# A hybrid attention block on one core: two gate parts moved ahead, four weight splits moved to GpSimd, weight scaling and late loads moved in the last stage

## The chip, the cores and the metric

The kernel runs on one core of a Trainium2 chip. The metric is the device time of one execution in microseconds. The kernel's text is Python that issues instructions to five engines: TensorE (PE, products), VectorE (DVE, `V` in the code), ScalarE (ACT, `A`), GpSimd (POOL, `G`) and SyncE (SP, `SY`), whose queue starts nearly all DMAs. All data is fp32.

## The reference

One layer of a diffusion backbone over 512 latent tokens of width 1024, with 256 context tokens.

```python
mod = silu(c) @ w_ada + b_ada
sh1, sc1, gt1, sh2, sc2, gt2 = split(mod, 6)
h = modulate(rms_norm(x, norm1_g), sh1, sc1)
mix = merge_branches(o_mla @ w_br_mla, gla_branch(o_gla, gr, ...), gate_logits, w_out)
x = x + gt1 * mix                         # the two branches: latent attention, gated linear attention
h = modulate(rms_norm(x, norm2_g), sh2, sc2)
val, gate = split(h @ w_up, 2)            # d_ff = 2816
hid = gelu(conv3x3(gate)) * val
x = x + gt2 * (hid @ w_down)
return rms_norm(x, final_g)
```

`gt2`, the "second gate", is the last sixth of the modulation vector: 1024 numbers, each a sum over the 1024 rows of a column of `w_ada`.

## The kernel before

**Split products.** Each fp32 operand is kept as two tiles of a rounded type, a high part `h` and the rest `l`. `split(hi, lo, src, eng)` makes them: a cast on ScalarE (`A.copy`, the CAST rows), then a subtraction `lo = src - hi` on `eng`, GpSimd by default and VectorE where `V` is given. `mm3` multiplies with three products. A weight goes by DMA into a `raw` (or `rawd`) tile, is split into `whi` and `wlo` (or into two `s4` tiles, named `s`), and is then used by TensorE.

**Order of the work.** From the linear attention on, a planner fixes each engine's order ahead of time: the text's order gives priority, and the planner puts an instruction where it expects its operands and buffers to be ready. On the chip each engine then runs its list strictly in order. `tc.issue_after(ins)` holds the instructions of a block behind `ins` on the queue of `ins`; `load[0]` is the last weight load that was marked so.

**The stages around the change.**

- *Linear attention* (pool `eg`, 217 to 408 us): four heads `h`. Each makes decays, states, output and gate on VectorE and ScalarE while TensorE runs the projections. In between come `mod_begin` and `mod_end` (other sixths of the modulation: two 512 KB loads and eight multiply-adds on VectorE each) and the first half of the merge, `merge_mla(j)`, for j = 0 to 7; the last head does `merge_mla(6)` and `merge_mla(7)`.
- *Merge* (pool `em_`, from 408 us): for j = 0 to 7 the second half of the merge, with weights loaded one step ahead by `merge_weights`; some of `w_out` is loaded here (`load_wo`), and the first gate `gt1` is made.
- *`w_out` and the second norm*: `w_out_norm(t)` for four token tiles t: 48 products of width 512, then on VectorE `xn = p * gt1`, `x += xn` in two halves, the sum of squares on ScalarE, the root, and `xn = x * r`. `transposed(t, n)` turns that `xn` on TensorE and modulates it.
- *Up projection and convolution* (559 to 772 us), per block of 128 columns: two projections, nine convolution steps on VectorE (`ac<-pb,cwT,ac`), gelu, product.
- *Last stage* (from 772 us): NP = 9 pairs of blocks of `w_down` in a seven-product scheme, the sums of weights having been written to device memory earlier (`ws`). A first loop over n makes four of the products from `wa` and `wb` (two splits each), a second one (`back`, with `back_weights(n)`) the other three. The last NL = 4 blocks are multiplied plainly by weights that `load_down` scales by `gt2` beforehand (`raw<-raw,gt`). `x2`, stored in device memory after `w_out_norm`, is loaded again and the result added; `fg` is the gain of the final norm.

**The second gate.** `gt2` is a 128 x 1024 tile, zero but for the bias in row 0. `gate_part(j)` adds 256 columns to it: two loads of 512 KB into `wa` tiles (two buffers) and eight multiply-adds `gt<-wa,csilu,gt` on VectorE, so 8 loads and 32 multiply-adds in all for the four parts. In the up projection, at i = 12, TensorE sums it over the partitions. Parts 0 and 1 stand in the merge (at j = 6 and after the last `load_wo`), part 2 after `w_out_norm(0)`, part 3 after `w_out_norm(1)`:

```python
n0 = w_out_norm(0)
gate_part(2)
n1 = w_out_norm(1)
gate_part(3)
transposed(0, n0)
n0 = w_out_norm(2)
```

Of the kernel before, what the change touches and what calls it, by code (L numbers as in the profile page):

```python
# [9 lines left out]
F32 = mybir.dt.float32  # L10
# [3 lines left out]
ALU = mybir.AluOpType  # L14
# [9 lines left out]
NF = FF // 128  # L24
NL = 4
# [47 lines left out]
def block_kernel(ctx: ExitStack, tc: tile.TileContext, p, out):  # L73
# [80 lines left out]
    def k3(t_, k, n):  # L154
        return t_[:, 0:k * n].rearrange("p (k n) -> p k n", k=k)
# [150 lines left out]
    def mod_begin(tile_, acc=None):  # L306
        begun.append(mod_part(3072 + len(begun) * 256, mp_tile() if acc is None else acc, tile_))
# [782 lines left out]
    gt1 = S4([128, 1024], F32)  # L1090
    G.dma_start(out=gt1, in_=p["b_ada"][0:1, 2048:3072].broadcast_to([128, 1024]))

    with tc.tile_pool(name="egl", bufs=1) as eg:
        smask = LF[:, 768:1024].bitcast(mybir.dt.bfloat16)
        pinned.add("G")
# [170 lines left out]
        def gate_out(h, on, gr):  # L1266
            tp = pb()
            for t in range(4):
                cs = slice(t * 128, (t + 1) * 128)
                PE.transpose(tp[:, cs], on[:, cs], ident)  # L1270
            V.scalar_tensor_tensor(out=gr, in0=tp, scalar=col("gla_norm_g", 0), in1=gr, op0=ALU.mult, op1=ALU.mult)
            yT[h] = S4([128, 2, 512])
            split(yT[h][:, 0, :], yT[h][:, 1, :], gr, V)

        def merge_mla(j):
            wga = split_w(load_cols(w_in, CGA + j * 128))
            ga = pb()
            proj(wga, ga)
            sg = tl(eg, [128, 512], F32, "sg", 1)
            sigmoid(sg, ga)  # L1280
            wbm = split_w(load_cols(w_brm, j * 128, k1=4), 512)
            bm = pb()
            for k in range(4):
                mm3(bm, k3(wbm[0], 4, 128)[:, k, :], k3(wbm[1], 4, 128)[:, k, :], oT[k][:, 0, :], oT[k][:, 1, :], k == 0,
                    k == 3)
            if j % 2 == 0:
                m1[j // 2] = S4([128, 2, 512], F32)
            tt(V, m1[j // 2][:, j % 2, :], bm, sg, ALU.mult)
# [13 lines left out]
        for h in range(GH):  # L1302
            St = states(h, dec)
            on = output(h, dec, Q, St)
            if h + 1 < GH:
                dec = decay(h + 1)
                merge_mla(2 * h)
                kq = proj_kq(h + 1)
                with tc.issue_after(key_end[0].ins):
                    mod_end()  # L1310
            else:
                merge_mla(2 * h)
                mod_end()
                mod_begin(S4f)
                merge_mla(2 * h + 1)
            gate_out(h, on, gr)
            if h + 1 < GH:
                Q = apply(kq, dec)
                gr = gate(h + 1)
                to_tokens(dec, Q)  # L1320
                mod_begin(S4f)
                merge_mla(2 * h + 1)
# [4 lines left out]
    hbm = ctx.enter_context(tc.tile_pool(name="hbm", bufs=1, space=bass.MemoryType.DRAM))  # L1327
    x2_ = [tl(hbm, [128, 1024], F32, f"x2_{t}") for t in range(4)]
    sums_ = [tl(hbm, [128, 2048], F32, f"ws_{i}") for i in range(NP)]
    gate_ = ctx.enter_context(tc.tile_pool(name="gate", bufs=1))  # L1330
    gt2 = tl(gate_, [128, 1024], F32, "gt2")
    V.memset(gt2, 0.0)
    SY.dma_start(out=gt2[0:1, :], in_=p["b_ada"][0:1, 5120:6144])
    emf_ = tc.tile_pool(name="emf", bufs=1)
    emf = emf_.__enter__()
    x2 = [tl(emf, [128, 1024], F32, f"x2{t}") for t in range(4)]
# [22 lines left out]
    with tc.tile_pool(name="emg", bufs=1) as em_:  # L1359
# [3 lines left out]
        def mraw():  # L1363
            return tl(em_, [128, 1024], F32, "xn", 3)


        def gate_part(j):
            acc = gt2[:, j * 256:j * 256 + 256]
            for k0 in (0, 4):
                r3 = k3(tl(em_, [128, 1024], F32, "wa", 2), 4, 256)  # L1370
                SY.dma_start(out=r3, in_=w_ada[:, k0:k0 + 4, 5120 + j * 256:5376 + j * 256])
                for k in range(4):
                    V.scalar_tensor_tensor(out=acc, in0=r3[:, k, :], scalar=csilu[:, k0 + k:k0 + k + 1], in1=acc,
                                           op0=ALU.mult, op1=ALU.add)

        gsum = p2()
        ahead = merge_weights(0)
        for j in range(8):
            wgb, wbg = ahead
            gb = pb()  # L1380
            proj(wgb, gb)
            if j + 1 < 8:
                ahead = merge_weights(j + 1)
            bg = pb()
            for k in range(4):
                bg_ = mm3(bg, k3(wbg[0], 4, 128)[:, k, :], k3(wbg[1], 4, 128)[:, k, :], yT[k][:, 0, :], yT[k][:, 1, :], k == 0,
                    k == 3)
            sg = tl(em_, [128, 512], F32, "sg", 2)
            si = sigmoid(sg, gb)
            tt(V, sg, bg, sg, ALU.mult)  # L1390
            tt(V, sg, sg, m1[j // 2][:, j % 2, :], ALU.add)
            mg[j] = S4([128, 2, 512])
            split(mg[j][:, 0, :], mg[j][:, 1, :], sg, V)
            ahead_ = load[0].ins
            if j in (1, 2, 3, 5):
                load_wo(len(wo), mraw)
            if j == 0:
                mod_end()
            with tc.issue_after(ahead_):
                if j < 4:  # L1400
                    mod_part(2048 + j * 256, gsum[:, j * 256:j * 256 + 256], mraw)
                elif j == 4:
                    mod_begin(mraw, p2()[:, 0:256])
            if j == 6:
                m_, gh, gl = mp_tile(), *[tl(em_, [128, 1024], F32R, "xn", 3) for _ in range(2)]
                with tc.issue_after(si.ins):
                    A.copy(m_, begun[7])
                    A.copy(gh, gsum)
                sub(V, gl, gsum, f(gh))
            elif j == 7:  # L1410
                with tc.issue_after(bg_.ins):
                    mod_fin(7, m_)
                    gp = p2()
                    for half in range(2):
                        hs = slice(half * 512, (half + 1) * 512)
                        total(gp[:, hs], gh[:, hs], gl[:, hs])
                        tt(V, gt1[:, hs], gt1[:, hs], gp[:, hs], ALU.add)
            if j == 6:
                with tc.issue_after(load[0].ins):
                    gate_part(0)  # L1420
        for k in range(4, 8):
            load_wo(k)
        with tc.issue_after(load[0].ins):
            gate_part(1)
        h2h = [S4([128, 2, 512]) for _ in range(4)]
        h2l = [S4([128, 2, 512]) for _ in range(4)]
        def w_out_norm(t):
# [31 lines left out]


        n0 = w_out_norm(0)
        gate_part(2)
        n1 = w_out_norm(1)
        gate_part(3)
        transposed(0, n0)
        n0 = w_out_norm(2)
        transposed(1, n1)
# [24 lines left out]
    with tc.tile_pool(name="eff", bufs=1) as ef:  # L1492
# [104 lines left out]

        def back_weights(n):
            r = back_raw(n)
            SY.dma_start(out=r, in_=w_down[:, 2 * n + 1, :])  # L1600
            w = back_hl(n)
            split(*w, r, V)
            if n % 2 == 0:
                k = min(2, NP - n)
                r = back_raw(n)
                for i in range(k):
                    SY.dma_start(out=r[:, 512 * i:512 * i + 512], in_=sums_[n + i][:, 1024:1536])
                h_, l_ = back_hl(n)
                split(h_[:, 0:512 * k], l_[:, 0:512 * k], r[:, 0:512 * k], V)
                t4[0] = h_, l_  # L1610
            h_, l_ = S4([128, 768]), S4([128, 768])
            split(h_, l_, second[n], V)
            return w, t4[0], (h_, l_)
# [6 lines left out]
        for n in range(NP):  # L1620
            r = raw_()
            SY.dma_start(out=r[:, 0:512], in_=w_down[:, 2 * n, 0:512])
            SY.dma_start(out=r[:, 512:1024], in_=sums_[n][:, 1536:2048])
            wa = split_w(r, eng=V)
            r = raw_()
            SY.dma_start(out=r, in_=sums_[n][:, 0:1024])
            wb = split_w(r, eng=V)
            a, z = n == 0, n == NP - 1
            product(p1, first[n], 0, wa, 0, a, z)
            product(p6, first[n], 768, wa, 512, a, z)  # L1630
            product(p7, first[n], 512, wb, 512, a, z)
            product(p5, first[n], 256, wb, 0, a, z)
            if n in (2, 4, 6, 8):
                r = load_down(NF - NL + n // 2 - 1)
                wl_.append((S4([128, 1024]), S4([128, 1024])))
                split(*wl_[-1], r, V)
            if n == NP - 3:
                bw.append(back_weights(0))
# [20 lines left out]
                    product(p3, w[2], 256, w[0], 512, n == 0, z)  # L1659

        x2 = [S4f() for _ in range(4)]
        for t in (2, 3, 0, 1):
            SY.dma_start(out=x2[t], in_=x2_[t])
        SY.dma_start(out=fg, in_=p["final_g"].rearrange("(a b) -> a b", a=1).broadcast_to([128, 1024]))
        for n in range(NP):
            if n:
                bw.append(back_weights(n))
            if n < NP - 2:
                back(n, (2, 4, 3), bw[n])
        for x in (2, 4, 3):  # L1670
# [110 lines left out]
```

## Time and profile before

| | |
|---|---|
| median of 3 runs | 893.69 us (892.61 to 893.79) |
| the profiled execution | 892.85 us |
| its span, first to last instruction | 891.1 us |
| mean granted TensorE clock | 0.993 |
| busy: TensorE, weight loads, VectorE, ScalarE, GpSimd | 869.7, 738.1, 642.8, 412.2, 374.0 us |
| DMA | 130.53 MB, 146 GB/s on average |

Rows of the profile name tiles by the program's names without numbers, as out<-in: `gt` is a gate tile, `wa` a gate part's weights, `xn` a scratch tile of the merge, `p` and `pb` tiles of the product memory. A releaser is what ended an engine's idle time. Several helpers record their instructions under one line, L90, so a row is told apart by its tiles and its time. A product's end in the trace is modelled; starts are what to go by.

### The profile page before, as it was taken

What the parts mean: (1) busy time and instruction counts of PE and PEld (TensorE: products, weight loads), DVE (VectorE), ACT (ScalarE), POOL (GpSimd) and SP (SyncE); (2) the same over time, 40 slices, a digit from 0 to 9 for tenths busy, and PEclk for the clock granted to TensorE, in tenths of its full rate; (3) what the DMA queues carried; (4) which work ended last, traced back from release to release, by engine and by line L of the source; (5) the groups of instructions that cost most, each with busy time, mean ns of one, the idle gap of its engine ahead of it and who ended that gap; (6) DMA issues with size and microseconds to landing.
All of it is one profiled execution on the core that took longest, in us unless ns stands there. A gap on an engine that the chain in (4) does not pass through costs nothing.

```text
span 891.1 us, 12819 instructions
## 1 busy us (share of the span) xinstructions
PE 869.7 (98%) x4794; PEld 738.1 (83%) x4794; DVE 642.8 (72%) x1054; ACT 412.2 (46%) x666; POOL 374.0 (42%) x253
## 2 busy tenths in 40 slices
PE   7999999999999999999999899999999999999996
PEld 5788899888888888888888689888888888877785
DVE  4477788876978686845775984986677666877867
ACT  4355676773454645433544333433334333356514
POOL 2512355460624343423743422877768776000005
PEclk9999999999999999999999899999999999999998
DMA  9960001225414242427982930756546755467702
GB/s 292 319 178 1 1 4 34 72 69 168 106 40 133 55 131 58 119 80 262 266 267 91 278 104 17 235 168 194 190 155 195 232 168 193 144 201 275 255 13 95
DMA packets 141648, 130.53 MB, mean 146 GB/s; under 512 B 7947, under 2 KB 122995, under 8 KB 141586
## 3 DMA queue, kind: packets, MB, share of 16 engines
q1 hardware_dynamic: 140354, 126.67, 46.4%
q10 hardware_dynamic: 832, 2.40, 0.7%
q8 instruction: 37, 0.61, 0.3%
q0 software_dynamic: 400, 0.65, 0.2%
q14 instruction: 25, 0.20, 0.1%
HBM read 115.87 MB, written 13.63 MB: 145 GB/s over the span
## 4 chain that ended last, share of the span: by engine, by line
PE 80%; DVE 7%; DMA 6%; ACT 4%; issue 2%; POOL 1%; SPq 0%; DVEq 0%; ACTq 0%; POOLq 0%
PE pb L90 42%; PE p L90 17%; PE pb L89 14%; PE p L89 6%; DMA raw<-in_w_ada_dram 2%; DVE s L90 2%; ACT s L90 2%; DMA wa<-in_w_ada_dram 1%; DVE gt L90 1%; DMA s<-ws 1%; DVE wlo L90 1%; DMA xn<-in_w_ada_dram 1%; ACT P L90 1%; DVE mx L90 0%; POOL s L90 0%
## 5 line engine op out<-in xcount | busy, mean ns | idle before, releaser
L90 POOL TENSOR_TENSOR wlo<-raw,whi 128x1024 fp32r<-128x1024 f32 (+1 forms) x88 | 200.7, 2290 | 226.5 <-ACT whi L90 193.2
L90 PE MATMUL pb<-s,whi 128*128 128x512 f32 (+1 forms) x906 | 271.3, 382 | 0.0
L90 PEld LDWEIGHTS pb<-s,whi 128*128 128x128 f32 x906 | 167.3, 188 | 32.3
L90 PE MATMUL pb<-s,wlo 128*128 128x512 f32 (+1 forms) x453 | 172.7, 381 | 0.0
L90 ACT CAST whi<-raw 128x1024 fp32r<-128x1024 f32 (+1 forms) x105 | 101.8, 973 | 126.2 <-PE pb L90 49.1
L90 DVE SCALAR_TENSOR_TENSOR ac<-pb,cwT,ac 128x441 f32<-128x441 f32 (+2 forms) x160 | 110.9, 694 | 11.4 <-ACT ac L90 7.4
L89 PE MATMUL pb<-s,whi 128*128 128x512 f32 x320 | 101.2, 394 | 0.0
L90 PEld LDWEIGHTS pb<-s,wlo 128*128 128x128 f32 x453 | 85.2, 188 | 16.3
L90 PE MATMUL p<-s,s 128*128 128x512 f32 (+1 forms) x398 | 86.8, 371 | 1.0 <-DVE s L90 0.9
L90 PEld LDWEIGHTS p<-s,s 128*128 128x128 f32 x398 | 68.4, 193 | 14.5 <-DVE s L90 2.0
L89 PEld LDWEIGHTS pb<-s,whi 128*128 128x128 f32 x320 | 59.3, 188 | 11.5
L89 PE MATMUL pb<-s,wlo 128*128 128x512 f32 x160 | 62.8, 392 | 0.0
L90 POOL TENSOR_TENSOR s<-s,edge 128x512 f32<-128x512 f32 x7 | 12.1, 1759 | 114.7 <-ACT s L90 114.7
L90 PE MATMUL p<-whi,s 128*128 128x512 f32 x168 | 56.3, 394 | 0.0
L90 PE MATMUL pb<-whi,s 128*128 128x512 f32 x164 | 53.7, 390 | 0.0
L90 ACT ACTIVATE ac<-ac 128x512 f32<-128x512 f32 x22 | 13.9, 632 | 77.5 <-DVE ac L90 77.5
L90 PE MATMUL pb<-s,s 128*32 128x128 f32 (+2 forms) x340 | 46.3, 319 | 0.9 <-DMA s<-in_w_ada_dram 0.9
L90 DVE TENSOR_TENSOR pl<-pb,ph 128x512 fp32r<-128x512 f32 x48 | 33.0, 687 | 13.0 <-ACT ph L90 12.5
L90 PE MATMUL p<-kT,s 128*128 128x512 f32 (+1 forms) x192 | 41.2, 350 | 0.9 <-ACT P L90 0.9
L90 PEld LDWEIGHTS pb<-s,s 128*128 128x128 f32 (+1 forms) x340 | 36.1, 159 | 6.8 <-DVE rv L90 1.3
L90 PE MATMUL p<-s,whi 128*128 128x256 f32 (+1 forms) x156 | 38.6, 338 | 0.0
L90 ACT CAST ph<-pb 128x512 fp32r<-128x512 f32 x48 | 28.2, 587 | 20.7 <-PE pb L90 20.5
(274 smaller groups left out, 1667.6 us busy)
## 6 DMA issues: line engine op xcount, KB each, us to landing
raw<-in_w_up_dram SPq DMA_DIRECT2D x44, 512.0 KB, 5.9
raw<-in_w_in_dram SPq DMA_DIRECT2D x28, 512.0 KB, 4.1
rawd<-in_w_down_dram SPq DMA_DIRECT2D x21, 512.0 KB, 5.8
s<-in_w_ada_dram SPq DMA_DIRECT2D x20, 512.0 KB, 6.3
ws<-rawd SPq DMA_DIRECT2D x18, 512.0 KB, 5.6
raw<-in_w_ada_dram SPq DMA_DIRECT2D x10, 512.0 KB, 7.6
xn<-in_w_ada_dram SPq DMA_DIRECT2D x10, 512.0 KB, 4.8
raw<-in_w_down_dram SPq DMA_DIRECT2D x9, 512.0 KB, 4.4
```

The source lines that it names most:

```text
L89: return fn(*args, **kw)
L90: ins = fn(*args, **kw)
```

## The change

The gate's zeroing (now on GpSimd), bias load and `gate_part` move ahead of the linear attention, and `gate_part` takes the pool for its `wa` tiles. Part 0 now stands in the last head between `mod_begin` and `merge_mla(7)`, part 1 behind `merge_mla(7)`, part 2 at j = 6 of the merge, part 3 after the last `load_wo`; none stands between the `w_out_norm` calls. In the last stage the low parts of `wa` and `wb` of the pairs 0 and 1 are made on GpSimd, `load_down` comes at the pairs 1, 2, 4, 5 instead of 2, 4, 6, 8, and the loads of `x2` and `fg` come after `back_weights(5)` (NP - 4 = 5) instead of before the second loop.

```diff
+    gate_ = ctx.enter_context(tc.tile_pool(name="gate", bufs=1))
+    gt2 = tl(gate_, [128, 1024], F32, "gt2")
+    G.memset(gt2, 0.0)
+    SY.dma_start(out=gt2[0:1, :], in_=p["b_ada"][0:1, 5120:6144])
+
+    def gate_part(j, pool):
+        acc = gt2[:, j * 256:j * 256 + 256]
+        for k0 in (0, 4):
+            r3 = k3(tl(pool, [128, 1024], F32, "wa", 2), 4, 256)
+            SY.dma_start(out=r3, in_=w_ada[:, k0:k0 + 4, 5120 + j * 256:5376 + j * 256])
+            for k in range(4):
+                V.scalar_tensor_tensor(out=acc, in0=r3[:, k, :], scalar=csilu[:, k0 + k:k0 + k + 1], in1=acc,
+                                       op0=ALU.mult, op1=ALU.add)
...
                 mod_begin(S4f)
+                with tc.issue_after(load[0].ins):
+                    gate_part(0, eg)
                 merge_mla(2 * h + 1)
+                with tc.issue_after(load[0].ins):
+                    gate_part(1, eg)
...
-    gt2 = tl(gate_, [128, 1024], F32, "gt2")
-    V.memset(gt2, 0.0)
-    SY.dma_start(out=gt2[0:1, :], in_=p["b_ada"][0:1, 5120:6144])
...
             if j == 6:
                 with tc.issue_after(load[0].ins):
-                    gate_part(0)
+                    gate_part(2, em_)
         for k in range(4, 8):
             load_wo(k)
         with tc.issue_after(load[0].ins):
-            gate_part(1)
+            gate_part(3, em_)
...
         n0 = w_out_norm(0)
-        gate_part(2)
         n1 = w_out_norm(1)
-        gate_part(3)
         transposed(0, n0)
...
         def back_weights(n):
             r = back_raw(n)
-            SY.dma_start(out=r, in_=w_down[:, 2 * n + 1, :])
+            load[0] = SY.dma_start(out=r, in_=w_down[:, 2 * n + 1, :])
...
-            wa = split_w(r, eng=V)
+            wa = split_w(r, eng=G if n < 2 else V)
             r = raw_()
             SY.dma_start(out=r, in_=sums_[n][:, 0:1024])
-            wb = split_w(r, eng=V)
+            wb = split_w(r, eng=G if n < 2 else V)
...
-            if n in (2, 4, 6, 8):
-                r = load_down(NF - NL + n // 2 - 1)
+            if n in (1, 2, 4, 5):
+                r = load_down(NF - NL + len(wl_))
                 wl_.append((S4([128, 1024]), S4([128, 1024])))
                 split(*wl_[-1], r, V)
...
-        for t in (2, 3, 0, 1):
-            SY.dma_start(out=x2[t], in_=x2_[t])
-        SY.dma_start(out=fg, in_=p["final_g"].rearrange("(a b) -> a b", a=1).broadcast_to([128, 1024]))
         for n in range(NP):
             if n:
                 bw.append(back_weights(n))
+            if n == NP - 4:
+                with tc.issue_after(load[0].ins):
+                    for t in (2, 3, 0, 1):
+                        SY.dma_start(out=x2[t], in_=x2_[t])
+                    SY.dma_start(out=fg, in_=p["final_g"].rearrange("(a b) -> a b", a=1).broadcast_to([128, 1024]))
```

More of the change, by code (lines that the diff above doesn't have):

```diff
@@ L1329, in block_kernel @@
     sums_ = [tl(hbm, [128, 2048], F32, f"ws_{i}") for i in range(NP)]
-    gate_ = ctx.enter_context(tc.tile_pool(name="gate", bufs=1))
-    gt2 = tl(gate_, [128, 1024], F32, "gt2")
-    V.memset(gt2, 0.0)
-    SY.dma_start(out=gt2[0:1, :], in_=p["b_ada"][0:1, 5120:6144])
     emf_ = tc.tile_pool(name="emf", bufs=1)
@@ L1364, in mraw @@
             return tl(em_, [128, 1024], F32, "xn", 3)
[L1367 to L1374, printed above, removed]
         gsum = p2()
```

## The prediction

> **What bounds the kernel now.** I read the page first, then TensorE's own waits, then TensorE's and VectorE's timelines around the longest of them, then the windows for the granted clock.
>
> ```profile
> span 891.1 us, 12819 instructions
> PE 869.7 (98%) x4794; PEld 738.1 (83%) x4794; DVE 642.8 (72%) x1054; ACT 412.2 (46%) x666; POOL 374.0 (42%) x253
> ```
>
> TensorE is busy for 869.7 of 891.1 us. The change alters no product, so it can only gain where TensorE waits or runs at a lower clock, and it can lose at any place where TensorE does not wait now. The waits, from the view by releaser: the first row is of the whole run, the next three of the window from 750 us on.
>
> ```profile
> PE pb L90 <- DVE xn L90: 3.7, 1, 3.7
> ...
> PE p L90 <- DVE wlo L90: 0.8, 1, 0.8
> PE p L90 <- DVE s L90: 0.4, 1, 0.4
> PE pb L90 <- DVE wlo L90: 0.2, 1, 0.2
> ```
>
> One wait stands out, 3.7 us for `xn`, the normalised token tile that `transposed(0, n0)` turns. The three last-stage waits make 1.4 us. TensorE's timeline around the long one (start, length, tiles, count, idle before), one row of the chain for an undisturbed rate, and the windows (busy of PE, PEld, DVE, ACT, POOL, then clock, DMA share, GB/s):
>
> ```profile
> 475.47 5.60 PE L90 MATMUL p<-s,s 128*128 128x512 f32 x24
> ...
> 481.38 23.11 PE L90 MATMUL p<-s,s 128*128 128x512 f32 x100
> 508.19 1.97 PE L90 MATMUL pb<-cst,xn 128*128 128x128 f32 x8 [3.71 <-DVE xn L90]
> 509.81 11.10 PE L90 MATMUL p<-s,s 128*128 128x512 f32 x39
> 520.75 1.03 PE L90 MATMUL pb<-cst,xn 128*128 128x128 f32 x8
> ...
> 564.66 108.83 PE pb L90 x480
> ...
> 500.00:510.00 10.00, 6.29 (x29) 5.19 (x28) 9.82 (x17) 2.40 (x5) 3.21 (x2) 0.86 0.84 255
> 510.00:520.00 10.00, 10.00 (x37) 8.10 (x37) 9.89 (x27) 4.05 (x9) 0.00 (x0) 0.80 0.33 104
> ```
>
> The wait costs twice. After it the granted clock is 0.86 and 0.80. An undisturbed product takes 108.83/480 = 0.227 us; the 39 after the wait take 520.75 - 509.81 = 10.94 us instead of 39 x 0.227 = 8.84, and the 8 transposes 1.97 us instead of the 1.03 of the next eight. That is 2.1 + 0.9 = 3.0 us of slow clock, so this place costs 3.7 + 3.0 = 6.7 us. VectorE is 98 to 99% busy there. Its timeline:
>
> ```profile
> 488.70 4.13 DVE L90 SCALAR_TENSOR_TENSOR gt<-wa,csilu,gt 128x256 f32<-128x256 f32 x8
> ...
> 493.95 2.09 DVE L90 TENSOR_TENSOR x<-x,xn 128x512 f32<-128x512 f32 x1
> 496.98 1.60 DVE L90 SCALAR_TENSOR_TENSOR gt<-wa,csilu,gt 128x256 f32<-128x256 f32 x1 [0.95 <-DMA wa<-in_w_ada_dram]
> 498.50 2.88 DVE L90 TENSOR_TENSOR x<-x,xn 128x512 f32<-128x512 f32 x1
> ...
> 507.40 0.74 DVE L90 TENSOR_SCALAR xn<-x,rr 128x1024 f32<-128x1024 f32 x1
> ...
> 508.65 0.68 DVE L90 TENSOR_TENSOR x<-x,xn 128x512 f32<-128x512 f32 x1
> ...
> 489.00:514.00 25.00, 13.63 (x23) 0.00 (x0) 0.86 0.93 270
> ...
> 493.07 7.75 POOL L90 TENSOR_TENSOR wlo<-raw,whi 128x1024 fp32r<-128x1024 f32 x3 [8.04 <-ACT whi L90]
> ```
>
> The reader sees the gate's multiply-adds (`gt<-wa`) threaded through the chain that makes `xn`; the window row, of the instructions on `gt` alone, gives them 13.63 of 25 us (23 of them). The first eight are `gate_part(1)`, the rest parts 2 and 3. While GpSimd splits (493 to 501 us), VectorE's operations on two SBUF tiles are slow: 2.09 and 2.88 us for one that takes 0.68 after it.
>
> **The change part by part.**
>
> *Gate parts out of the `w_out_norm` calls.* After the change one part stands before `w_out_norm(0)`, where part 1 stands now (the eight at 488.70 stay), and none between the calls. Sixteen multiply-adds and four 512 KB loads leave this stretch. So `xn` comes sooner: the `x` update that ended at 496.0 is followed at once by the second, 0.68 to 2.88 us, ending at 496.7 to 498.9. From the squares to `xn` I take the undisturbed chain of `w_out_norm(3)`:
>
> ```profile
> 530.94 1.06 ACT L90 ACTIVATE xn<-x 128x1024 f32<-128x1024 f32 x1 [6.05 <-DVE x L90]
> ...
> 533.34 0.76 DVE L90 TENSOR_SCALAR xn<-x,rr 128x1024 f32<-128x1024 f32 x1
> ```
>
> 534.1 - 530.9 = 3.2 us, and 0.2 for the two hand-overs between engines, an estimate from the 0.05 us between the end of `xn` at 508.14 and the transposes: `xn` stands ready at 500.1 to 502.3. TensorE's queue as it is reaches the transposes at 508.19 - 3.71 = 504.5, so with this order the wait is gone with 2 to 4 us to spare. But the order is written by a planner, which with less vector work may put the transposes further ahead. Two calls have 96 products, so 24 + 100 - 96 = 28 products of `w_out_norm(2)` stand before the transposes now, 6.4 us; if all of them go behind, TensorE is there at 498.1 and waits 2.0 to 4.2 us. Bounds of the remaining wait: 0 and 4.2, with up to 3.0 of slow clock. I take 2.0. The planner's order was 3.7 us too early over a chain with four slow operations: 2.09, 2.88, 1.60 and 2.23 (the longest of the multiply-adds, in the row by tile below) make 8.8 us where 0.68, 0.68 and twice that row's median of 0.49 make 2.3, so 6.5 too much. The two that stay have 3.6 of that, and 3.7 x 3.6/6.5 = 2.0. I charge no slow clock for 2.0: of the two waits here that are nearest in size, 3.7 had it and the 0.8 us below had not (clock 1.00 from 780 to 790), and the bounds keep it. Term: -6.7 + 2.0 = -4.7, between -6.7 and +0.5.
>
> [...]
>
> *Parts 0 and 1 into the last head of linear attention.* Sixteen multiply-adds on VectorE, four 512 KB loads on SP's queue, two new `wa` buffers there:
>
> ```profile
> L90 DVE SCALAR_TENSOR_TENSOR gt<-wa,csilu,gt x32: 472/485/2227, 461.1 to 516.0; 128x256 f32<-128x256 f32 x32
> ...
> 390.00:400.00 10.00, 10.00 (x59) 8.71 (x57) 2.02 (x7) 3.96 (x8) 2.38 (x1) 1.00 0.07 21
> 400.00:410.00 10.00, 10.00 (x49) 8.32 (x49) 7.71 (x16) 3.69 (x6) 4.52 (x3) 1.00 0.57 173
> ```
>
> 16 x 0.49 = 7.8 us against 10.3 us of idle VectorE from 390 to 410; DMA is 7% and 57% busy. I cost it at nothing. If the cover is gone, one multiply-add stuck behind GpSimd (2.23 us at most) ahead of a state update can hold TensorE once: 0 to +2.2. What queues behind the new loads on SP is the merge stage's weights, the slower rival below. A gain is excluded here, since TensorE is busy for 10.00 of 10 us in both rows. Parts 2 and 3 take the places of parts 0 and 1 with the same instructions: nothing. The memset and the bias row go ahead of the stage, onto GpSimd and SP:
>
> ```profile
> 226.33 7.35 POOL L90 TENSOR_TENSOR wlo<-raw,whi 128x1024 fp32r<-128x1024 f32 x3 [29.88 <-ACT whi L90]
> ...
> 411.69 0.91 DVE L90 MEMSET gt<- 128x1024 f32 x1 [0.35 <-DVE s L90]
> ```
>
> GpSimd is idle for 29.88 us there, which covers it; without cover it would be the memset's 0.91 us.
>
> *Last stage.* The four splits of pairs 0 and 1 go from VectorE to GpSimd, and the scaled weights (load, multiply, split) from pairs 2, 4, 6, 8 to 1, 2, 4, 5:
>
> ```profile
> L90 POOL TENSOR_TENSOR wlo<-raw,whi 128x1024 fp32r<-128x1024 f32 x70 | 177.4, 2539 | 168.2 <-ACT whi L90 134.8 <-PE pb L89 30.4 <-ACT rr L90 2.9
> ...
> 869.85 4.54 POOL L90 TENSOR_TENSOR s<-s,edge 128x512 f32<-128x512 f32 x1 [113.13 <-ACT s L90]
> ...
> 780.83 1.22 DVE L90 TENSOR_TENSOR wlo<-rawd,whi 128x1024 fp32r<-128x1024 f32 x1
> 782.09 0.50 PE L90 MATMUL p<-wlo,s 128*128 128x512 f32 x1 [0.79 <-DVE wlo L90]
> ...
> 780.00:790.00 10.00, 9.21 (x41) 7.26 (x40) 7.53 (x10) 7.25 (x8) 0.00 (x0) 1.00 0.53 157
> 820.00:830.00 10.00, 9.34 (x40) 7.03 (x39) 10.00 (x12) 6.59 (x9) 0.00 (x0) 1.00 0.78 262
> ```
>
> VectorE is relieved of 4 x 1.22 = 4.9 us ahead of 780 and given 2 x 1.22 = 2.4 for the weight that moves to pair 1; GpSimd takes 4 x 2.5 = 10.2 us out of an idle stretch of 113. The split that TensorE waited for at 780.83 comes some 2.5 us sooner, and 0.79 goes. At pair 8, where VectorE is 100% busy (820 to 830), 2.4 us leave, more than the 0.2 and 0.4 of wait there; I take 0.5 of 0.6. Term: -1.3, between -1.4 and +2.5 (one split on GpSimd in the way).
>
> *x2 and the final gain later.* Five loads move behind the back weights of pair 5.
>
> ```profile
> 824.70 2.31 SPq L90 DMA_DIRECT2D s<-x  x4
> ...
> 864.14 0.69 DVE L90 TENSOR_TENSOR s<-s,s 128x512 f32<-128x512 f32 x1
> ```
>
> They issue at 824.70 now, whatever their place in the text, and are wanted at 864.14: 39 us of cover. Nothing; if it went, each late us would be one us at the end.
>
> **Sum.** Profiled execution 892.85 us (span 891.1): 892.85 - 4.7 - 1.3 = 886.85, so 886.9. That execution is 0.84 us under the median of the runs, 893.69.
>
> **The rivals.** *The wait stays.* The planner puts the transposes right behind `w_out_norm(1)`; at 498.1 plus 3.7 or so `xn` is still late, the clock drops again, and only the last stage gains: 892.85 - 1.3 = 891.5. For it: the planner was too early before. Against: what made it late is mostly gone.
>
> *GpSimd gets in VectorE's way in the last stage.* The rows 2.88 against 0.68 speak for it: a split on GpSimd holds back a vector operation on two SBUF tiles, and the pair splits and `raw<-raw,gt` are of that kind. One such delay of 2.5 us on the path instead of the gain: 892.85 - 4.7 + 2.5 = 890.7. Against: the convolution's operations, which read PSUM, are most of VectorE's work there. [...]
>
> *Slower: SP's queue.* The second part's loads wait on SP for the `wa` buffers of the first, so for vector work; behind them stand the first merge weights.
>
> ```profile
> 377.63 0.37 SPq L90 DMA_DIRECT2D raw<-in_w_in_dram  x1
> ...
> 408.70 0.71 PE L90 MATMUL pb<-s,whi 128*128 128x512 f32 x2
> ...
> raw<-in_w_in_dram SPq DMA_DIRECT2D x28, 512.0 KB, 4.1
> ```
>
> A load takes 4.1 us, a cast about 1.1 (as the squares of the same width above) and a split on GpSimd 2.5: issued by 401 it is in time for 408.7, and now it issues at 377.63, 23 us of cover. If the first part were done only at 407, TensorE would wait 6 us and lose 3.0 of clock: 892.85 - 6.0 + 9.0 = 895.9. It decides from about 404 on.
>
> **How the numbers follow.** Forecast 0.58, the wait stays 0.17, GpSimd in the way 0.15, SP's queue 0.10. The measurement tells apart some 0.2%, 1.8 us: faster is under 891.9. The forecast and GpSimd's case are nearly all under it, the wait that stays half: faster 0.76, same 0.13, slower 0.11. Alone the forecast reaches from 884.0 (all of 6.7 and 1.4, and 0.8 for what the memset and quieter DMA may give) to 889; the range takes in the two cases up to 891.5: 884.0 to 892.0, leaving out the last 0.10 and little else.
>
> **What would show it.** Right: no wait for `xn` of over 2.5 us, clock 1.00 from 500 to 520, no `gt<-wa` between the `x` updates, and sixteen of them at 365 to 410 with TensorE unbroken. Waits for `wlo` under 0.5 us from 770 to 830. Wrong: a clock under 1.00 near 500, a new TensorE wait at 385 to 415, a SP issue of the first merge weights after 401, or splits of 2.5 us and more on VectorE at 760 to 790.

## The result and the profile after

The changed kernel takes 897.78 us in the median of seven runs (896.11 to 899.99), against 893.79 us for the kernel before beside it: a ratio of 1.0045, with an interval of 1.0029 to 1.0060. It is 4 us slower, where 886.9 was forecast. The profiled execution took 896.73 us. The head of its page, and TensorE's waits over the whole run:

```profile
span 894.9 us, 12819 instructions
...
PE 869.8 (97%) x4794; PEld 738.8 (83%) x4794; DVE 644.3 (72%) x1049; ACT 412.7 (46%) x666; POOL 386.4 (43%) x258
...
PE pb L90 <- DVE ac L90: 5.0, 2, 3.8
...
PE p L90 <- DVE wlo L90: 2.1, 1, 2.1
...
PE pb L90 <- DVE xn L90: 1.2, 1, 1.2
PE pb L90 <- ACT whi L90: 0.7, 1, 0.7
```

TensorE does the same work (869.8 us against 869.7). The wait for `xn` has shrunk from 3.7 to 1.2 us. In its place stand two waits for `ac`, the convolution's tile, which the kernel before did not have, and a longer one for `wlo`. TensorE's timeline at these places, then the windows:

```profile
504.47 1.09 PE L90 MATMUL pb<-cst,xn 128*128 128x128 f32 x8 [1.21 <-DVE xn L90]
...
760.40 0.82 PE L90 MATMUL pb<-s,whi 128*128 128x512 f32 x2 [3.82 <-DVE ac L90]
...
782.28 0.50 PE L90 MATMUL pb<-whi,s 128*128 128x512 f32 x1 [1.20 <-DVE ac L90]
...
805.23 0.79 PE L90 MATMUL p<-wlo,s 128*128 128x512 f32 x1 [2.10 <-DVE wlo L90]
...
500.00:510.00 10.00, 8.79 (x44) 7.09 (x43) 6.54 (x14) 3.27 (x10) 3.81 (x2) 1.00 0.83 259
510.00:520.00 10.00, 10.00 (x50) 8.37 (x49) 10.00 (x27) 5.97 (x13) 2.90 (x1) 1.00 0.13 52
...
750.00:760.00 10.00, 6.58 (x30) 5.11 (x28) 4.47 (x7) 0.00 (x0) 2.09 (x1) 1.00 0.63 220
760.00:770.00 10.00, 9.60 (x35) 7.81 (x36) 8.04 (x11) 3.70 (x5) 5.20 (x2) 0.83 0.33 98
...
800.00:810.00 10.00, 7.91 (x28) 6.10 (x27) 7.19 (x7) 4.94 (x5) 0.00 (x0) 0.83 0.79 256
```

The clock (the third number from the end) is now 1.00 from 500 to 520 us, where it was 0.86 and 0.80, and 0.83 in two stretches of the up projection and the last stage, where it was 1.00. The kernel before has there:

```profile
760.00:770.00 10.00, 10.00 (x46) 8.29 (x45) 8.44 (x11) 3.54 (x5) 0.00 (x0) 1.00 0.43 146
...
800.00:810.00 10.00, 10.00 (x45) 7.99 (x44) 5.77 (x6) 5.56 (x6) 0.00 (x0) 1.00 0.83 291
```

To see what each place is worth, take TensorE's position in both traces: the start of the product that has the same amount of product work before it. The changed kernel is 0.6 us behind from about 45 us on (a load at the start came later; experiments without that delay have the same parts), 4.9 ahead from 530 to 755 us, 0.8 behind at 770, 1.9 at 800, 5.6 at 810, and 4.1 behind from 830 us to the end. So 5.5 us were gained where the gate's parts left, and 9.0 us were lost between 755 and 830 us. At 760 us it is 3.82 of waiting and 3.41 us at half clock, which costs 1.7; at 805 us it is 2.10 and again 1.7.

What the 3.82 us wait for is in VectorE's and SP's lists:

```profile
747.96 2.89 DVE L90 SCALAR_TENSOR_TENSOR ac<-pb,cwT,ac 128x441 f32<-128x441 f32 x4 [0.94 <-ACT ac L90]
756.23 1.23 DVE L90 TENSOR_TENSOR rawd<-rawd,gt 128x1024 f32<-128x1024 f32 x1 [5.39 <-DMA rawd<-in_w_down_dram]
757.38 2.88 DVE L90 SCALAR_TENSOR_TENSOR ac<-pb,cwT,ac 128x504 f32<-128x504 f32 x4
...
742.66 1.01 SPq L90 DMA_DIRECT2D ws<-rawd  x2
...
748.22 0.32 SPq L90 DMA_DIRECT2D rawd<-ws  x1
750.29 0.33 SPq L90 DMA_DIRECT2D rawd<-in_w_down_dram  x1
...
ws<-rawd SPq DMA_DIRECT2D x2, 512.0 KB, 6.3
```

The multiply of pair 1's scaled weight stands between the fourth and the fifth of a block's eight convolution steps on VectorE (the ninth, `ac<-pb,pcol,cwT`, is ScalarE's). VectorE took up nothing behind it and stood still for 5.39 us, and with it the steps that read the tile of the product memory (PSUM) which TensorE needs for the next block: the last of them ends at 757.38 + 2.88 = 760.26 us, and TensorE starts at 760.40. The load had issued only at 750.29, behind the stores of the last weight sums from the `rawd` tiles; the waits of SP's own queue from 738 to 760 us name these stores for 3.2 us in two waits. The second stall has another such multiply ahead of the split that TensorE waits for:

```profile
802.81 1.23 DVE L90 TENSOR_TENSOR raw<-raw,gt 128x1024 f32<-128x1024 f32 x1 [3.17 <-DMA raw<-in_w_down_dram]
803.95 1.22 DVE L90 TENSOR_TENSOR wlo<-rawd,whi 128x1024 fp32r<-128x1024 f32 x1
```

In the kernel before these multiplies waited as well, as a grouped row of its VectorE from 735 to 880 us says (busy, mean ns, idle before). Three of the four stood behind the convolution; the first, at 772.06, stood between its last steps and waited 1.17 us:

```profile
L90 DVE TENSOR_TENSOR raw<-raw,gt 128x1024 f32<-128x1024 f32 x4 | 4.9, 1226 | 10.4 <-DMA raw<-in_w_down_dram 10.4
```

4.9 us of work came with 10.4 us of waiting. In their old places it cost at most the 1.4 us that TensorE waited from 750 us on.

### The profile page after: what moved, and what is told of

Same layout as the page of the kernel before. It is cut to its first block, busy times and chain, and to the rows that moved or that the text cites. A ratio compares the mean times of both kernels' runs of the same rounds, so it can differ in the third digit from the quotient of the medians.

```text
span 894.9 us, 12819 instructions
## 1 busy us (share of the span) xinstructions
PE 869.8 (97%) x4794; PEld 738.8 (83%) x4794; DVE 644.3 (72%) x1049; ACT 412.7 (46%) x666; POOL 386.4 (43%) x258
## 4 chain that ended last, share of the span: by engine, by line
PE 73%; DMA 9%; DVE 7%; ACT 4%; POOL 3%; issue 3%; SPq 0%; DVEq 0%; POOLq 0%; ACTq 0%
PE pb L90 36%; PE p L90 17%; PE pb L89 14%; PE p L89 6%; POOL wlo L90 2%; DMA raw<-in_w_ada_dram 2%; DVE s L90 2%; DMA raw<-in_w_down_dram 2%; DMA rawd<-in_w_down_dram 1%; DMA raw<-in_w_up_dram 1%; ACT s L90 1%; DMA ws<-rawd 1%; DVE ac L90 1%; DVE gt L90 1%; DMA xn<-in_w_ada_dram 1%
## 5 line engine op out<-in xcount | busy, mean ns | idle before, releaser
L90 POOL TENSOR_TENSOR wlo<-raw,whi 128x1024 fp32r<-128x1024 f32 (+1 forms) x91 | 210.6, 2323 | 224.4 <-ACT whi L90 193.7
L90 PE MATMUL p<-s,s 128*128 128x512 f32 (+1 forms) x398 | 83.9, 364 | 0.6 <-DVE s L90 0.5
L90 POOL TENSOR_TENSOR s<-s,edge 128x512 f32<-128x512 f32 x7 | 10.4, 1502 | 99.0 <-ACT s L90 99.0
L90 PEld LDWEIGHTS pb<-whi,s 128*128 128x128 f32 x164 | 30.7, 188 | 9.0 <-DVE ac L90 1.6
```

The costliest lines, as they stand in the source:

```text
L90: ins = fn(*args, **kw)
```

## The experiments

Ratios are to the kernel before in the same set of runs, with 95% intervals.

**Which part loses.** Four kernels undo or isolate parts.

*e1_gate*: the kernel before with the two `gate_part` edits of the change, the last stage as it was.

> The kernel before with the gate's parts alone moved (0 and 1 into the last linear attention head, 2 and 3 into the merge, the memset on GpSimd); the last stage is that of before. In the trace of the changed kernel TensorE is 5.5 us ahead of before from 520 us on, up to 760 us. Theory W (the loss is all made in the last stage, by the scaled weights): those 5.5 us reach the end, 888.3 against 893.8. Theory P (GpSimd's splits of pairs 0 and 1 get in VectorE's way): the same 888.3, as there are none here. Rival R (the gain is not handed on: the last stage waits on transfers and gives it back whatever is edited there): 892 to 894.

Measured: 889.0 us, 0.9947 (0.9933 to 0.9962), 4.7 us faster. The gain reaches the end; R fell here.

*e2_gate_splits_x2*: the changed kernel with

```diff
-            if n in (1, 2, 4, 5):
-                r = load_down(NF - NL + len(wl_))
+            if n in (2, 4, 6, 8):
+                r = load_down(NF - NL + n // 2 - 1)
```

> The changed kernel with the scaled weights back at pairs 2, 4, 6 and 8; the GpSimd splits of pairs 0 and 1 and the later x2 loads stay. Theory W: the two long stalls (3.8 and 2.1 us of waiting and 1.7 us of half clock behind each) go with the weights, and the other waits for the convolution too: 887 to 888.5. Theory P: the splits keep the stalls, 893 to 898. Theory R: 892 to 894.

Measured: 887.43 us, 0.9930 (0.9911 to 0.9948). Putting the four scaled weights back brings 10.4 us.

*e3_weights*: the kernel before with only the opposite edit.

> The kernel before with the scaled weights alone moved to pairs 1, 2, 4 and 5; all splits of the pairs stay on VectorE, the gate's parts where they were. From 760 to 830 us the changed kernel lost 9.0 us against before (from 4.9 ahead to 4.1 behind). Theory W: slower by 6 to 10 us, 900 to 904, with a VectorE wait of 3 us or more for a scaled weight's load between convolution steps and a TensorE wait for ac behind it. Theory P: 893.8, no change. Theory R: no more than 1 us of change.

Measured: 899.48 us, 1.0067 (1.0052 to 1.0082), 6.0 us slower. VectorE's wait for pair 1's weight is there too:

```profile
760.45 1.23 DVE L90 TENSOR_TENSOR rawd<-rawd,gt 128x1024 f32<-128x1024 f32 x1 [3.17 <-DMA rawd<-in_w_down_dram]
```

*e4_splits*: the kernel before with `eng=G if n < 2 else V` in both `split_w` calls.

> The kernel before with the four splits of pairs 0 and 1 alone on GpSimd. Theory W: no loss; the 0.8 us wait for a split at 780 us goes and VectorE gets 4.9 us of room: 892.4 to 893.8. Theory P: the stalls are there, 899 to 903. Theory R: 893.8.

Measured: 892.23 us, 0.9982 (0.9970 to 0.9994), 1.6 us faster. P fell as the cause. The loss is the scaled weights', and larger in the changed kernel (10.4 us) than in e3, without the other parts of the change (6.0). In the changed kernel the multiply stands behind four of the block's convolution steps and waits 5.39 us; in e3 it stands behind six and waits 3.17, and TensorE's wait for `ac` behind it is 1.1 us instead of 3.82. Whether the splits on GpSimd or the gate's earlier parts make that difference, no run separates.

**What about the scaled weights.** Is it the multiply's place in VectorE's list (Q), or the loads and buffers (L)?

*e5_behind_conv*: the changed kernel, with the multiplies queued behind the last convolution step, whose instruction the text now keeps in `conv[0]`.

```diff
-            tt(V, r, r, gt2, ALU.mult)
+            with tc.issue_after(conv[0].ins):
+                tt(V, r, r, gt2, ALU.mult)
```

> The changed kernel with the multiplies of the scaled weights (raw<-raw,gt) queued on VectorE behind the last step of the last convolution; loads, buffers and pairs stay as changed. Theory Q (place in VectorE's queue: a multiply that waits for its load stands ahead of convolution steps that TensorE needs): the waits of 3.8 and 1.2 us for ac and the half clock behind the first go, some 6 us; the wait of 2.1 us at 805 us, whose multiply stands behind the convolution already, stays with its half clock: 890.5 to 892.5. Theory L (the earlier loads themselves: four 512 KB loads in the raw buffers' turn hold back the loads of the pairs, wherever the multiply stands): TensorE waits for whi or wlo instead, 895 to 898.

Measured: 891.01 us, 0.9963 (0.9947 to 0.9979), inside Q's numbers. With the same loads in the same buffers, only the place in the list changed, and 6.8 of the 10.4 us came back. Its trace differs from Q's account in one point: the wait of 2.1 us at 805 us, which was to stay, is gone too. The longest that are left are 1.39 us for `ac` and 1.22 for `wlo`, with no half clock behind them: the clock of the whole execution is 0.998, as in e14, which waits 0.6 us at most from 735 us on.

*e6_gpsimd*: the changed kernel with `tt(G, r, r, gt2, ALU.mult)` and `split(*wl_[-1], r, G)` for the scaled weights.

> The changed kernel with the multiply and the split of the four scaled weights on GpSimd, which stands idle from 778 us on; loads, buffers and pairs stay as changed. Theory Q: no engine that TensorE waits for stands behind those loads any more, all of the 9.0 us comes back: 886.5 to 889. Theory L: the loads come no sooner, 895 to 898. Theory P (GpSimd's work on two SBUF tiles slows VectorE's): eight more operations on GpSimd, slower pair splits on VectorE, 890 or more, with rows of over 2 us among VectorE's 1.22 us splits.

Measured: 894.82 us, 1.0016 (0.9992 to 1.0039): a miss for Q. The waits for `ac` are gone, and others have come. Rows of its VectorE, GpSimd and TensorE:

```profile
776.29 2.40 POOL L90 TENSOR_TENSOR raw<-raw,gt 128x1024 f32<-128x1024 f32 x1 [3.73 <-DMA raw<-in_w_down_dram]
778.65 2.36 POOL L90 TENSOR_TENSOR wlo<-rawd,whi 128x1024 fp32r<-128x1024 f32 x1
...
784.79 3.42 DVE L90 TENSOR_TENSOR wlo<-raw,whi 128x1024 fp32r<-128x1024 f32 x1
...
784.28 2.85 POOL L90 TENSOR_TENSOR s<-raw,s 128x1024 fp32r<-128x1024 f32 x1
...
781.06 0.51 PE L90 MATMUL pb<-wlo,s 128*128 128x512 f32 x1 [1.79 <-POOL wlo L90]
```

Beside a GpSimd split of 2.85 us, a VectorE split that takes 1.22 elsewhere took 3.42, so what P speaks of is there in this trace.

But a slow VectorE split is not what TensorE waits for. From 735 us on it waits 0.30 us for one, 3.9 for two casts on ScalarE that had waited for loads, and 1.79 for a split on GpSimd. How far the slow splits held back those loads, no run shows. The GpSimd split stands behind the multiply at 776.29, which had waited 3.73 us for its load: the fault has moved to GpSimd, whose list stood still behind it instead. (This execution, 897.7 us, also holds a wait of 1.86 us for `mp` at 236.56, in a stage that the edit leaves alone; of the experiments only e10's trace has it too.)

*e7_pair1*: the changed kernel with the scaled weights at `(1, 4, 6, 8)`.

> The changed kernel with the scaled weights at pairs 1, 4, 6 and 8: only the first stands earlier than before, the others where they were. Theory Q: the stall at 760 us alone is left (3.8 us and 1.7 of half clock; 5.7 in the positions), and 887.4 of the kernel with all four back becomes 892.5 to 893.5. If the weights at pairs 2 and 5 carry most of it: 888 to 889.

Measured: 896.76 us, 1.0034 (1.0019 to 1.0050). The one weight at pair 1 makes 9.3 of the 10.4 us, more than Q said. In the trace (898.94 us, 2.2 above the median) 3.8 us are lost ahead of the multiply, by another wait for `ac` of 1.97 us at 748.24 and half clock behind it (0.43 us a product instead of 0.23), so not all of its 9.3 need be the multiply's. The rows at the multiply:

```profile
760.18 1.23 DVE L90 TENSOR_TENSOR rawd<-rawd,gt 128x1024 f32<-128x1024 f32 x1 [5.44 <-DMA rawd<-in_w_down_dram]
...
764.35 0.70 PE L90 MATMUL pb<-s,whi 128*128 128x512 f32 x2 [3.37 <-DVE ac L90]
```

*e8_gpsimd_2468*: the GpSimd edit of e6 on the kernel of e2.

> The gate's move, the GpSimd splits and the later x2 loads, the scaled weights at pairs 2, 4, 6 and 8 as before, but their multiply and split on GpSimd. Theory Q: the waits that are left in the last stage with the weights on VectorE (3.1 us in three) go too: 884 to 886.5. Theory P: GpSimd slows VectorE, 888 or more. Theory L: as with the weights on VectorE, 887.4.

Measured: 890.42 us, 0.9960 (0.9938 to 0.9983), 3 us above e2's 887.43, though the two intervals overlap a little. GpSimd is no better engine for these weights in the old places, and probably a worse one.

**What pair 1's multiply waits for.**

*e9_noload1*: the changed kernel, pair 1's load left out.

```diff
-            SY.dma_start(out=r, in_=w_down[:, k, :])
-            tt(V, r, r, gt2, ALU.mult)
+            if k > NF - NL:
+                SY.dma_start(out=r, in_=w_down[:, k, :])
+            tt(V, r, r if k > NF - NL else gt2, gt2, ALU.mult)
```

> The changed kernel without the load of pair 1's scaled weight: its multiply reads the resident gate tile instead, into the same buffer; multiply, split and products stay, so only the transfer that VectorE waits for is left out (and that weight's values with it). Theory Q: the multiply waits for nothing wherever it stands among the convolution steps, no wait for ac over 1.5 us and no half clock near 760 us; the stalls of the pairs behind may stay: 890.5 to 893. Rival (the multiply and split themselves are too much for VectorE between convolutions, or the buffer turn is): 895 to 898.

Measured: 897.74 us, 1.0042 (1.0016 to 1.0068). Nothing came back: as "it waits for its load", Q fell. VectorE, SP and TensorE in its trace:

```profile
753.03 3.05 DVE L90 TENSOR_TENSOR rawd<-gt 128x1024 f32<-128x1024 f32 x1 [4.47 <-DMA raw<-in_w_down_dram]
...
756.61 5.80 DVE L90 SCALAR_TENSOR_TENSOR ac<-pb,cwT,ac 128x441 f32<-128x441 f32 x8
...
745.59 1.01 SPq L90 DMA_DIRECT2D ws<-rawd  x2
...
762.55 1.19 PE L90 MATMUL pb<-s,whi 128*128 128x512 f32 x2 [4.16 <-DVE ac L90]
```

A multiply without any load still stood 4.47 us. The transfer named beside it is one into another buffer and not its operand; what it needs is the `rawd` tile that it writes, and the stores from the `rawd` tiles had issued at 745.59, 7.4 us before. Pair 1's scaled weight is the fifth tile of the `raw_` turn, the second `rawd`, and that one still holds the last weight sums. The run does not price the load alone: without it the planner put the multiply further ahead, before all eight steps of the block, and it took 3.05 us there instead of 1.23.

*e13_nobuf*: buffer, load and multiply of that weight left out together; the resident gate tile is split in its stead.

```diff
-                r = load_down(NF - NL + len(wl_))
+                if n == 1:
+                    raws[0] += 1
+                r = gt2 if n == 1 else load_down(NF - NL + len(wl_))
```

> The changed kernel with pair 1's scaled weight replaced by the resident gate tile, split directly: load, multiply and buffer of that one weight are left out (its values with them), cast, subtraction and products stay. Theory B (the multiply at 760 us waits for its rawd buffer, which still holds the last weight sums while they are stored, 6.3 us, and only then for its load; TensorE waits for the convolution steps behind it): no wait for ac over 1.5 us and clock 1.00 near 760 us, 890.5 to 893. Rival W (the cast and subtraction of a fifth weight this early are what is too much): 896 to 898.

Measured: 891.0 us, 0.9969 (0.9944 to 0.9995), B's numbers. The two windows that lost most are whole again:

```profile
750.00:760.00 10.00, 10.00 (x46) 8.29 (x45) 7.33 (x12) 3.67 (x6) 5.20 (x3) 1.00 0.82 259
760.00:770.00 10.00, 10.00 (x46) 8.29 (x45) 7.37 (x11) 4.62 (x6) 5.20 (x3) 1.00 0.35 108
```

*e14_pairs2345*: the changed kernel with `if n in (2, 3, 4, 5):`, four early weights, none at pair 1.

> The changed kernel with the scaled weights at pairs 2, 3, 4 and 5: all four still early, but none takes a rawd buffer before the stores of the weight sums are done. Theory B: pair 1 alone made the loss near 760 us and what follows from it; 887.5 to 890. Rival (scaled weights before pair 6 cost in any case): 893 to 897.

Measured: 888.63 us, 0.9932 (0.9905 to 0.9959), as B said. One number in the text separates it from the changed kernel: from pair 2 on, early scaled weights cost nothing that these runs show. In this trace TensorE's waits from 735 us on are a single row:

```profile
PE p L90 <- DVE wlo L90: 1.0, 2, 0.6
```

*e15_no_x2*: the kernel of e2 with the `x2` and final gain loads as before.

> The gate's move and the GpSimd splits alone: the scaled weights at pairs 2, 4, 6 and 8, and the x2 and final gain loads where they were. The first gave 0.9947 and the second 0.9982 alone, 0.9929 together if they add, 887.6; with the later x2 loads on top it was 887.4. If the later loads are worth nothing, as forecast: 887 to 888.5. If they matter: 1 us or more apart from 887.4.

Measured: 887.77 us, 0.9932 (0.9901 to 0.9963), the same as with the later loads.

**Versions meant to be better still.** Three edits on the kernel of e2: *e10_behind_conv_2468* holds the multiplies behind the convolution (the edit of e5), *e11_sums* moves the last pair's two sums to GpSimd (`sub(V if 0 < n < NP - 1 else G, ...)` twice in `weight_sums`), *e12_both* does both.

> The gate's move, the GpSimd splits and the later x2 loads, scaled weights at pairs 2, 4, 6 and 8, their multiplies queued behind the last convolution step. Theory Q: the one multiply that stands ahead of the last convolution without the edge cost nothing in the one profile (its load had landed), so little changes in the median, 886 to 888; without the risk of a late load the spread (884.8 to 889.7) is smaller.

> The gate's move, the GpSimd splits and the later x2 loads, scaled weights at pairs 2, 4, 6 and 8 on VectorE; the two subtractions of the last pair's weight sums, where VectorE waits 3 to 4 us for a load between convolution steps in most profiles, go to GpSimd. Theory Q says that this is the same fault in another place: the waits for ac near 747 us (1.1 us) go: 885.5 to 887. Rival: GpSimd's sums come later and hold back the stores and loads of the last sums: 888 or more.

> Both edits together: the multiplies behind the last convolution step, and the last pair's two subtractions on GpSimd. Theory Q: 885 to 887, the lowest of all; no TensorE wait for ac from 735 us on.

Measured: 890.7 us, 0.9960 (0.9938 to 0.9982); 890.07 us, 0.9952 (0.9930 to 0.9975); 892.31 us, 0.9985 (0.9962 to 1.0007). The expectations of e10 and e12 missed, and e11 fell into its rival's numbers (888 or more). None beats e2; e11's interval overlaps e2's (0.9911 to 0.9948). For e10 the traces say part of why. A split on VectorE, a load on SP and a wait of TensorE, first in e2:

```profile
775.72 1.22 DVE L90 TENSOR_TENSOR wlo<-rawd,whi 128x1024 fp32r<-128x1024 f32 x1
...
776.96 0.33 SPq L90 DMA_DIRECT2D rawd<-in_w_down_dram  x1
...
799.81 0.50 PE L90 MATMUL pb<-wlo,s 128*128 128x512 f32 x1 [0.54 <-DVE wlo L90]
```

and in e10:

```profile
778.92 1.23 DVE L90 TENSOR_TENSOR wlo<-rawd,whi 128x1024 fp32r<-128x1024 f32 x1 [1.39 <-ACT whi L90]
...
780.17 0.33 SPq L90 DMA_DIRECT2D rawd<-in_w_down_dram  x1
...
801.93 0.50 PE L90 MATMUL pb<-wlo,s 128*128 128x512 f32 x1 [2.07 <-DVE wlo L90]
```

With the multiply held back the split behind it starts 3.2 us later; it frees the buffer of the next load, which issues 3.2 us later; and some 20 us on TensorE waits 2.07 us where it waited 0.54, with products of 0.43 us instead of 0.23 behind it. In TensorE's position e10 loses some 3 us more than e2 between 790 and 810 us. But e10's trace lacks e2's wait of 1.06 us for `ac` at 747.10, and of the 3.3 us between these two executions 1.8 stood before 735 us, most of it from a wait of 1.91 us for `mp` at 237.18, where the two kernels are the same. So the held-back multiply explains only part of e10's median. Why e11 gains nothing stays open.

The best versions are e2, e15 and e14 at 0.9930 to 0.9932, some 6 us below the kernel before; the runs don't tell them apart.

## Why the prediction was wrong, by its own steps

*Gate parts out of the `w_out_norm` calls: right, size included.* Forecast -4.7; the edit alone gave 4.7 us by the ratio of e1. That the size fits so well is in part luck: at its place the move gained 5.5 us, and e1's trace gives 1.4 of them back at 775 us, where TensorE waits 1.45 us for `wlo`. The remaining wait was taken as 2.0 and is 1.21 (0.9 in e1). The planner did put the transposes ahead: TensorE reached them at 504.47 - 1.21 = 503.26 instead of 504.48 us, far less than the 6.4 us allowed for. No slow clock followed, as charged: 1.00 from 500 to 520 us.

*Parts 0 and 1 into the last head: right in the cost, not in where the cover lay.* It was looked for from 390 to 410 us; the sixteen multiply-adds ran from 365.2 to 391 us with TensorE busy for 10.00 of 10 us in each window from 360 to 420, and the first merge weights issued at 378.81 instead of 377.63, so the rival of SP's queue did not arise. Other work of VectorE slid into 390 to 410 (13.3 us busy, 9.7 before):

```profile
L90 DVE SCALAR_TENSOR_TENSOR gt<-wa,csilu,gt x16: 471/485/2507, 365.2 to 391.0; 128x256 f32<-128x256 f32 x16
...
378.81 0.37 SPq L90 DMA_DIRECT2D raw<-in_w_in_dram  x1
```

*x2 and the final gain later: right, with one row misread.* e15 against e2 shows no cost. But the row at 824.70 holds four of the five loads. The fifth, of the final gain, stood elsewhere in the kernel before and is at 825.94 after:

```profile
748.39 1.18 SPq L90 DMA_DIRECT2D edge<-in_final_g_dram  x1
```

*Last stage: wrong; this step decides.* It said "VectorE is relieved of 4 x 1.22 = 4.9 us ahead of 780 and given 2 x 1.22 = 2.4 for the weight that moves to pair 1". The first half held: the splits alone are worth 1.6 us (e4), near the 1.3 of the term. The second half priced the moved weight by its two operations alone. It asked neither for its load and buffer at the new place, nor what stands behind the multiply on VectorE there: convolution steps, whose PSUM tiles TensorE waits for. In that place it cost 9.2 to 9.3 us (the changed kernel against e14, e7 against e2) where 2.4 of hidden work was charged. The upper bound of +2.5 was "one split on GpSimd in the way", again a duration and not a wait; a bound from the row of 10.4 us above, which stood in the trace of before, would have reached past the result. The price of the moved step should have been: buffer free (stores from 742.66, 6.3 us), load (750.29 to 756.2), multiply, and all of VectorE's list behind it.

*The rivals.* The wait for `xn` did not stay. GpSimd in VectorE's way did not make this loss (e4), though e6 shows such a row, 3.42 against 1.22; the convolution's steps from PSUM took 656 to 745 ns in the changed kernel and 661 to 745 in the one before. The slower side had only SP's queue at the linear attention's end; the one that came true, a waiting multiply in front of the convolution, was not on the list.

*What stays open.* e13 stands 3.6 us above e2; its longest wait from 735 us on is this one, which e14 does not have:

```profile
798.52 0.50 PE L90 MATMUL p<-wlo,s 128*128 128x512 f32 x1 [1.59 <-DVE wlo L90]
```

It belongs to the pairs behind pair 1 and e14 has early weights at those pairs too. What of the buffers' turn makes it, no run shows.

## What to carry to other kernels

A step that is moved earlier brings its buffer and its load along: price it by when its buffer comes free at the new place, plus the load, and then ask what stands behind it in its engine's list, which here stood still for 5.39 us. The wait in the trace before (10.4 us of idle against 4.9 of work) is the price to use as soon as the cover goes. Leaving a load out while its buffer stays shows whether the wait is the buffer's; look in the trace whether the instruction kept its place, which e9's did not.

## What the runs showed of the hardware

*The granted clock after a wait.* In the kernel before, a stretch of half clock (0.50) began at 507.22 us, 2.74 us into the wait of 3.71, and lasted 6.83 us. In the changed kernel there were two such stretches ahead of the last microseconds of the span, of 3.41 us each: from 760.83, which is 0.43 us after the end of the wait of 3.82, and from 805.20, at the end of the wait of 2.10. So the second wait cost 1.7 us on top.

The experiments' rows show it by the time from one product to the next, 0.23 us undisturbed. It was 0.43 behind the waits of 4.16 us at 762.55 in e9, 2.07 at 801.93 in e10 and 1.97 at 748.24 in e7. It stayed at 0.23 behind e7's longer wait of 3.37 at 764.35 and behind the 1.39 at 748.70 in e5, and the clock stayed at 1.00 behind the 1.21 at 504.47 in the changed kernel. Among these waits length alone does not tell which one costs clock: 1.97 did and 3.37 did not. What else decides, no run separates. The prediction's "3.7 had it and the 0.8 us below had not" was too coarse to say what a wait of 2.0 us would cost.
